# One transformer layer on one core: latent tokens first in the opening stage, adaLN rows and Strassen sums arranged otherwise, projection pieces dealt out otherwise

## The chip, the cores and the metric

One core of a Trainium2 chip runs the whole layer in one program. The metric is the device time of one execution in microseconds (us). The kernel before takes 1133.83 us (median of 3 runs, 1131.55 to 1134.39). About 0.3% (3.4 us) is what a measurement of this kernel can tell from no change.

## The reference, cut to what matters

```python
mod = silu(c) @ w_ada + b_ada                       # 1024 -> 6*1024; mod_c the same with c_ctx
sh1, sc1, gt1, sh2, sc2, gt2 = split(mod, 6)
hc = modulate(rmsnorm(ctx, g_pre_mix), csh1, csc1)  # 256 context tokens
hl = modulate(rmsnorm(x, g_pre_mix), sh1, sc1)      # 1024 latent tokens, width 1024
# hc, hl @ w_in -> z_q z_k z_v z_dec z_og z_f z_rx z_rg
#   states of the context: GLA (k, v, decay) and RG-LRU (conv of z_rx)
#   latents: bidirectional chunked GLA from those states | 2-D DFT of z_f | conv + RG-LRU of z_rx
x = x + gt1 * rmsnorm(yl @ w_out, g_post_mix)
hf = modulate(rmsnorm(x, g_pre_ffn), sh2, sc2)
x = x + gt2 * rmsnorm((silu(hf @ w_gate) * (hf @ w_up)) @ w_down, g_post_ffn)   # d_ff = 2816
```

All of it is float32. `modulate(h, sh, sc)` is `h * (1 + sc) + sh`.

## The kernel before, in words

Nearly all large products run as three float32r matmuls (`mm3`, lines 84 to 86): both operands are split into a rounded part (ScalarE cast) and a remainder (VectorE or GpSimd subtraction). The activations of the latents, normalised and modulated, stay in SBUF transposed, as `hl` (rounded and remainder, two halves of 512 tokens, 8 blocks of 128 features).

**Opening stage.** `ada_half` (L145) loads the shift and scale columns of `w_ada` in two halves of eight 512 KB loads each (pieces of 2 KB), multiplies them with the two conditioning vectors in four column groups of TensorE, and `columns` (L194) turns the result into per-feature columns. The context comes first: its k and v projections (`zkc`, `zvc`) and conv input (`zc`) run between the two halves. Then the first 512 latent tokens are modulated (`mod_half`), then the second 512, and the projections v, k, rx of the latents follow (`z_v0`, `z_k`, `z_rx`).

**Middle stage.** `gla_states(p)` makes the chunk states of a pair of heads; `gla_block(p, n)` is one of eight blocks of 128 tokens. `fill(n, mark)` (L752) issues n pieces of a queue of q and f projections behind a marked TensorE instruction; a piece is six matmuls of 512 columns, a whole projection of 512 tokens four pieces. `rg_gates` and `rg_scan` are the RG-LRU, `fourier` the DFT, `z_og` the output gate.

**Rows.** `ada_row` (L664) makes 1024 values of `mod` on VectorE: one step (`ada_step`) is a load of 512 KB and one multiply-add over 128x1024; after eight steps TensorE sums the partitions, into a row replicated on all partitions (`row_ps`), or, for the FFN shift, into a column.

**Border to the FFN.** `x_product` multiplies with `w_out`, normalises, and gives `xn`; `x_transposed` transposes it to `hx`. The FFN's gate and up products use seven Strassen products: `sums(n)` builds the five operands s1, s2, s4, s3, a22 of token block n, each split by `put` (L931; two casts and two subtractions of 256 columns). `first(f)` does the two products of feature block f that need no sums (24 matmuls of 512 columns); `rest(f)` the other five (60), on weights prepared by `t_split`. `EARLY` blocks have their `first` before `rest(0)`. Feature blocks are 22; then `down` runs.

**Order.** The tile framework orders each engine's instructions by its own planned timeline, starting from program order; `tc.issue_after` adds an edge behind a given instruction. SBUF is 43 pages of 4 KB a partition (`pg`) and 13 half pages (`hp`), given out in program order.

Of the kernel before, what the change touches and what calls it, by code (L numbers as in the profile page):

```python
# [16 lines left out]
P = 128  # L17
# [21 lines left out]
def tile_trunk(ctx: ExitStack, tc: tile.TileContext, A: dict):  # L39
# [101 lines left out]
    sp2, sm4 = sm("sp2", 4), sm("sm4", 4)
    V.tensor_scalar_mul(sp2, sp, 2.0)
    V.tensor_scalar_mul(sm4, sp, -4.0)

    def ada_half(h):  # L145

        ps = (aux if h else mm)("ada_ps")
        for k in range(KB):
            raw = pg((P, 2, 512), name="ada_raw")
            load(raw, A["w_ada"][k * P:(k + 1) * P, 0:2 * D].rearrange("p (i n) -> p i n", i=2)[:, :, h * 512:(h + 1) * 512])  # L150
            for i in range(2):
                for j in range(2):
# [41 lines left out]
    def columns(h, ps):  # L194

        sb = hp((P, 256), name="ada_sb")
        S.copy(sb, ps[:, 0:256])
        pc = (aux if h else mm)("ada_pc")[:, 0:16].rearrange("p (m q) -> p m q", q=8)
        for m in range(2):
            PE.matmul(pc[:, m], sb[:, m * P:(m + 1) * P], sel, start=True, stop=True)  # L200
        pcv = pc.rearrange("p m (i j w) -> p i j m w", i=2, j=2)

        def col4(c0):
            return sml[:, c0 + 4 * h:c0 + 4 * h + 4].rearrange("p (j m) -> p j m", j=2).unsqueeze(3).to_broadcast([P, 2, 2, 2])

        Av, Bv = (t[:, 4 * h:4 * h + 4, :].rearrange("p (j m) w -> p j m w", j=2) for t in (Acol, Bcol))
        V.tensor_add(Av, pcv[:, 1], col4(S_BSC))
        V.scalar_tensor_tensor(Av, Av, 1.0, col4(S_GPM), op0=ALU.add, op1=ALU.mult)
        V.tensor_add(Bv, pcv[:, 0], col4(S_BSH))

    load(cm, A["cmat"])
    cb = [row_block(A["ctx"], i * P) for i in range(2)]
    ada_ps = ada_half(0)
    for xb in cb:
        norm(xb)
    cT = list(transposed(cb))
# [74 lines left out]

    raws = w_N_load([(C_V, 256), (C_DEC, 32)])
    columns(0, ada_ps)
    hc = [[pg((P, 4, TC), F32R, f"hc{s}{i}") for i in range(2)] for s in range(2)]

    def mod_c(h):
        return modulate(cT[4 * h:4 * h + 4], 1, lambda kk: hc[0][kk // 4][:, kk % 4, :], lambda kk: hc[1][kk // 4][:, kk % 4, :])

    mod_c(0)
    w_v = [w_N_split(raws, G)]  # L300
    w_k_raw = [w_T_load(C_K)]
    zvc = [mm("zvc") for _ in range(2)]
    zkc = [mm("zkc") for _ in range(2)]

    def v_c(ks):
        for m in range(2):
            for k in ks:
                mm3(zvc[m][:, 0:288], *(hc[s][k // 4][:, k % 4, m * P:(m + 1) * P] for s in range(2)), *w_v[0][k], k == 0, k == KB - 1)

    v_c(range(4))  # L310
    ada_ps = ada_half(1)
    w_k_raw.append(w_T_load(C_K + P))
    w_k = [split(r, (P, KB, P), eng=G) for r in w_k_raw]
    xb0 = [row_block(A["x"], i * P) for i in range(2)]
    columns(1, ada_ps)
    started = mod_c(1)
    v_c(range(4, KB))
    for p in range(2):
        z_c(w_k[p], range(KB), zkc[p])
    w_rx_raw = w_T_load(C_RX)  # L320
    xb0 += [row_block(A["x"], i * P) for i in range(2, 4)]


    wdec_raw, wdec = hp(name="wdec_raw"), hp((P, 512), F32R, "wdec")
    load(wdec_raw, A["wdec"])
    with tc.issue_after(started.ins):
        S.copy(wdec, wdec_raw)
        V.tensor_sub(wdec[32:64, :], wdec_raw[32:64, :], wdec[32:64, :].bitcast(F32))
        w_rx = [split(w_rx_raw, (P, KB, P))]
        for xb in xb0:  # L330
            norm(xb)
# [33 lines left out]
    for m in range(2):  # L365
        v0_parts(zdt_c, m, vNc[0][:, m, :], zvc[m])
# [1117 lines left out]
```

## Time and profile before

| | |
|---|---|
| median of 3 runs | 1133.83 us |
| the profiled execution, its span | 1134.18 us, 1132.4 us |
| TensorE busy | 1078.5 us, 95% |
| VectorE, ScalarE, GpSimd busy | 72%, 43%, 7% |
| mean granted TensorE clock | 0.979 |
| chain of waits: TensorE's share | 83% |

A busy TensorE is not at its peak: the windows of the trace count a matmul that waits in the pipeline, or runs at half the clock, as busy. A window therefore has to be read with its granted clock beside it.

### The profile page before, as it was taken

What the parts mean: (1) busy time and instruction counts of PE and PEld (TensorE: products, weight loads), DVE (VectorE), ACT (ScalarE), POOL (GpSimd) and SP (SyncE); (2) the same over time, 40 slices, a digit from 0 to 9 for tenths busy, and PEclk for the clock granted to TensorE, in tenths of its full rate; (3) what the DMA queues carried; (4) which work ended last, traced back from release to release, by engine and by line L of the source; (5) the groups of instructions that cost most, each with busy time, mean ns of one, the idle gap of its engine ahead of it and who ended that gap; (6) DMA issues with size and microseconds to landing.
All of it is one profiled execution on the core that took longest, in us unless ns stands there. A gap on an engine that the chain in (4) does not pass through costs nothing.

```text
span 1132.4 us, 15040 instructions
## 1 busy us (share of the span) xinstructions
PE 1078.5 (95%) x5547; PEld 900.1 (79%) x5547; DVE 810.4 (72%) x1370; ACT 490.2 (43%) x931; POOL 83.6 (7%) x93
## 2 busy tenths in 40 slices
PE   4899998999899999959999999999999999999997
PEld 2799896776689888838878888888888888888886
DVE  3474698477588466797879777768777668967794
ACT  3452675466373355663314332333323247554251
POOL 2210000103100011370000000000000000000100
PEclk8899999999999999979999999999999999999999
DMA  9802312222427222361283242424232468767572
GB/s 328 306 20 67 120 38 56 48 56 71 167 75 243 75 93 94 112 167 57 93 276 106 78 136 84 121 75 139 85 114 81 157 218 315 267 216 231 181 283 75
DMA packets 119970, 156.42 MB, mean 138 GB/s; under 512 B 8276, under 2 KB 70996, under 8 KB 119896
## 3 DMA queue, kind: packets, MB, share of 16 engines
q1 hardware_dynamic: 106536, 128.72, 34.9%
q10 hardware_dynamic: 13360, 26.75, 7.0%
q8 instruction: 43, 0.70, 0.3%
q14 instruction: 31, 0.25, 0.1%
HBM read 124.50 MB, written 28.57 MB: 135 GB/s over the span
## 4 chain that ended last, share of the span: by engine, by line
PE 83%; DVE 6%; DMA 4%; ACT 3%; issue 2%; POOL 1%; SPq 0%; DVEq 0%; POOLq 0%; ACTq 0%
PE prod L84 11%; PE prod L85 11%; PE prod L86 11%; PE dn L85 6%; PE dn L84 6%; PE dn L86 6%; PE z L84 3%; PE z L85 3%; PE z L86 3%; PE o_ps L85 3%; PE o_ps L86 3%; PE o_ps L84 3%; PE zn L85 3%; PE zn L86 3%; PE zn L84 2%; DMA wraw<-in_w_in 2%
## 5 line engine op out<-in xcount | busy, mean ns | idle before, releaser
L85 PE MATMUL dn<-dr,dl 128*128 128x512 f32 (+1 forms) x319 | 121.8, 382 | 0.0
L86 PE MATMUL dn<-dr,dl 128*128 128x512 f32 (+1 forms) x319 | 121.8, 382 | 0.0
L84 PE MATMUL dn<-dr,dl 128*128 128x512 f32 (+1 forms) x319 | 118.7, 382 | 0.0
L85 PE MATMUL zn<-w_lo,hl 128*128 128x256 f32 (+1 forms) x256 | 74.1, 292 | 0.0
L84 PE MATMUL zn<-w_hi,hl 128*128 128x256 f32 (+1 forms) x256 | 73.2, 289 | 0.0
L86 PE MATMUL zn<-w_hi,hl 128*128 128x256 f32 (+1 forms) x256 | 72.9, 288 | 0.0
L84 PE MATMUL prod<-a,b_hi 128*128 128x512 f32 x176 | 69.5, 395 | 1.4 <-ACT b_hi L91 1.4
L84 PEld LDWEIGHTS dn<-dr,dl 128*128 128x128 f32 x319 | 60.0, 188 | 11.7
L85 PE MATMUL prod<-a,b_hi 128*128 128x512 f32 x176 | 69.3, 393 | 0.0
L86 PEld LDWEIGHTS dn<-dr,dl 128*128 128x128 f32 x319 | 60.0, 188 | 11.7
L85 PEld LDWEIGHTS dn<-dr,dl 128*128 128x128 f32 x319 | 60.0, 188 | 11.5
L84 PE MATMUL prod<-s,wb_hi 128*128 128x512 f32 x176 | 68.9, 391 | 0.0
L86 PE MATMUL prod<-s,wb_lo 128*128 128x512 f32 x176 | 68.5, 389 | 0.0
L85 PE MATMUL prod<-s,wb_hi 128*128 128x512 f32 x176 | 68.5, 389 | 0.0
L86 PE MATMUL prod<-a,b_lo 128*128 128x512 f32 x176 | 67.9, 390 | 0.0
L84 PE MATMUL z<-hl,w_hi 128*128 128x512 f32 x160 | 65.5, 409 | 1.0 <-ACT on L605 1.0
L85 PE MATMUL z<-hl,w_hi 128*128 128x512 f32 x160 | 64.0, 400 | 0.0
L86 PE MATMUL z<-hl,w_lo 128*128 128x512 f32 x160 | 63.8, 399 | 0.0
L1189 ACT CAST dl<-h 128x512 fp32r<-128x512 f32 x77 | 47.8, 620 | 35.7 <-issue 20.6
L1190 DVE TENSOR_TENSOR dl<-h,dl 128x512 fp32r<-128x512 f32 x77 | 53.3, 692 | 13.6 <-ACT dl L1189 13.6
L1122 ACT CAST b<-wf_raw 128x512 fp32r<-128x512 f32 x22 | 13.7, 622 | 113.6 <-PE prod L86 105.7
L85 PE MATMUL o_ps<-wo_lo,yh 128*128 128x512 f32 x128 | 49.9, 392 | 0.0
(368 smaller groups left out, 2800.8 us busy)
## 6 DMA issues: line engine op xcount, KB each, us to landing
ada_raw<-in_w_ada SPq DMA_DIRECT2D x48, 512.0 KB, 6.3
h<-hd SPq DMA_DIRECT2D x77, 256.0 KB, 5.0
wd_raw<-in_w_down SPq DMA_DIRECT2D x77, 256.0 KB, 4.8
hd<-c ACTq DMA_DIRECT2D x55, 256.0 KB, 2.0
wf_raw<-in_w_gate SPq DMA_DIRECT2D x25, 512.0 KB, 3.9
wf_raw<-in_w_up SPq DMA_DIRECT2D x22, 512.0 KB, 4.4
wraw<-in_w_in SPq DMA_DIRECT2D x16, 512.0 KB, 4.6
xb<-in_x SPq DMA_DIRECT2D x8, 512.0 KB, 8.1
```

The costliest lines, as they stand in the source:

```text
L84: PE.matmul(out, lh, rh, start=start, stop=False)
L85: PE.matmul(out, lh, rl, start=False, stop=False)
L86: return PE.matmul(out, ll, rh, start=False, stop=stop)
L1122: S.copy(hi, u[:, 4:8])
L1189: S.copy(t[:, 0, :], raw)
L1190: V.tensor_sub(t[:, 1, :], raw, t[:, 0, :].bitcast(F32))
```

## The change: what it does

- The four blocks of the first 512 latents are loaded first, on ScalarE's queue. `w_ada`'s shift and scale columns come in eight parts of 2 x 512 KB, by feature block (pieces of 512 bytes instead of 2 KB), with the k and rx weights between them. For each feature block: transposes, `ada_part`, `columns`, `modulate`, and one block of depth of the four k and rx products of the first half. The context comes after the latents' second half.
- Four pieces of q and f stand behind each pair's keys; between the blocks of pair 0 there are 2, 1, 2, 1 ... where there were two each; pair 1 keeps one each.
- The FFN scale becomes a column, applied with the shift on ScalarE in the transposition; `xn` is made on ScalarE. The steps of the rows are placed otherwise, and the last row (gt2) moves from block 3 to blocks 10 and 11 of the FFN.
- `sums` works in place, in two steps first and two later, all subtractions on VectorE; six `first` stand before `rest(0)` instead of three. `y_block` uses half pages.

```diff
+    xb0 = [pg(name="xb") for _ in range(4)]
+    for i, xb in enumerate(xb0):
+        nc.scalar.dma_start(xb, A["x"][i * P:(i + 1) * P, :])
...
+    def ada_load(b):
+        raws = []
+        for i in range(2):
+            raw = pg((P, KB, P), name="ada_raw")
+            c = i * D + b * P
+            load(raw, A["w_ada"][:, c:c + P].rearrange("(k p) n -> p k n", p=P))
+            raws.append(raw)
+        return raws
+
+    def ada_part(raws):
+        ps = aux("ada_ps")
         for k in range(KB):
...
             for i in range(2):
+                g = 32 * (2 * i + k % 2)
+                PE.matmul(ps[g:g + 32, 0:P], s32[:, k, :], raws[i][:, k, :], start=k < 2, stop=k >= KB - 2)
...
+    a_raw, w4_raw = {0: ada_load(0)}, {0: w4_load(0)}
+    for b in range(1, KB):
+        a_raw[b] = ada_load(b)
+        if b % 2 == 0:
+            w4_raw[b // 2] = w4_load(b // 2)
+    v_raws = w_N_load([(C_V, 256), (C_DEC, 32)])
...
+    def z_block(b):
+        for (hi, lo), ps in zip(w4, z4):
+            mm3(ps, hi[:, b, :], lo[:, b, :], hl[0][0][b // 2][:, b % 2, :], hl[1][0][b // 2][:, b % 2, :], b == 0, b == KB - 1)
...
+    for b in range(KB):
+        kps = [next(x0_T)]
+        columns(b, ada_part(a_raw.pop(b)))
+        modulate(kps, 0, lambda kk: hl[0][0][kk // 2][:, kk % 2, :], lambda kk: hl[1][0][kk // 2][:, kk % 2, :])
+        if b:
+            z_block(b - 1)
+        if b % 2:
+            w4_split()
+    softplus()
+    w_v = [w_N_split(v_raws)]
+    z_block(KB - 1)
...
+    def scale_column(ps):
+        g8 = hp((P, P), name="g8")
+        load(g8[0:KB, :], A["g_pre_ffn"].rearrange("(k p) -> k p", p=P))
+        PE.transpose(ps[:, 16:16 + KB], g8[0:KB, :], ident[0:KB, 0:KB])
+        V.tensor_copy(sc2, ps[:, 16:16 + KB])
+        V.scalar_tensor_tensor(sc2, ps[:, 0:KB], 1.0, sc2, op0=ALU.add, op1=ALU.mult)
...
-        yield from ada_row(4 * D, times_row("g_pre_ffn", 1.0))
-        yield from ada_row(3 * D, None)
+        yield from ada_row(4 * D, scale_column, False)
+        yield from ada_row(3 * D, shift_column, False)
...
     with tc.issue_after(mid.ins):
         z_q(0, 1)
+    fill(4, mid)
     rg_ctx()
...
     for n in range(4):
-        fill(2, gla_block(0, n))
+        fill(2 - n % 2, gla_block(0, n))
...
-    fill(3, mid)
+    fill(4, mid)
...
     z_rg(1)
-    ada_step(9)
+    ada_step(8)
...
     fourier(zf[0], 0)
-    ada_step(0)
+    ada_step(1)
...
-            V.scalar_tensor_tensor(xn[:, hs], xr[:, hs], r2, sc2[:, hs], op0=ALU.mult, op1=ALU.mult)
+            S.mul(xn[:, hs], xr[:, hs], r2)
...
-                S.activation(x[:, kk, :], ps[:, k * P:(k + 1) * P], AF.Identity, bias=sh2[:, kk:kk + 1])
+                S.activation(x[:, kk, :], ps[:, k * P:(k + 1) * P], AF.Identity, bias=sh2[:, kk:kk + 1], scale=sc2[:, kk:kk + 1])
...
+        put("a22", n, a22)
+        V.tensor_add(a22, a21, a22)
+        put("s1", n, a22)
         yield
+        V.tensor_sub(a21, a11, a21)
+        V.tensor_sub(a11, a22, a11)
+        put("s2", n, a11)
         yield
-        G.tensor_sub(s4, a12, s2)
-        put("s4", n, s4)
-        yield
-        G.tensor_sub(s3, a11, a21)
-        put("s3", n, s3, G)
-        yield
-        put("a22", n, a22, G)
...
+        V.tensor_sub(a12, a12, a11)
+        put("s4", n, a12)
+        put("s3", n, a21)
...
-    EARLY = 3
-    all_of(sums(1))
+    EARLY = 6
+    for _ in range(2):
+        next(s01[1])
     first(0)
...
-        if f == 3:
-            for _ in ada_row(5 * D, times_row("g_post_ffn", 0.0)):
-                pass
-            gt2 = rows[2]
+        if f == 10:
+            last_row = ada_row(5 * D, times_row("g_post_ffn", 0.0))
+            for _ in range(KB):
+                next(last_row)
+        if f == 11:
+            all_of(last_row)
+            gt2 = rows[1]
```

## Rows read from the trace of the kernel before

**Rows 1.** Windows: busy us (instructions) of PE, PEld, DVE, ACT, POOL; clock, DMA, GB/s.

```profile
0.00:20.00 20.00, 8.02 (x82) 4.51 (x83) 6.05 (x34) 5.67 (x9) 1.95 (x8) 1.00 0.93 324
20.00:40.00 20.00, 13.29 (x110) 9.86 (x109) 3.21 (x14) 6.83 (x11) 8.18 (x5) 0.74 1.09 359
40.00:60.00 20.00, 17.92 (x130) 17.72 (x129) 14.91 (x31) 12.51 (x24) 4.77 (x5) 0.83 0.65 216
...
260.00:280.00 20.00, 18.00 (x99) 12.67 (x98) 12.23 (x31) 15.62 (x38) 6.26 (x6) 1.00 0.23 70
...
300.00:320.00 20.00, 15.38 (x59) 9.03 (x57) 10.52 (x10) 10.67 (x13) 0.00 (x0) 0.91 0.29 96
...
480.00:500.00 20.00, 14.62 (x56) 10.96 (x54) 19.82 (x24) 14.56 (x43) 18.14 (x16) 0.83 0.62 178
500.00:520.00 20.00, 11.44 (x44) 9.32 (x45) 18.36 (x26) 8.23 (x14) 6.23 (x4) 0.74 0.24 58
...
580.00:600.00 20.00, 19.25 (x80) 14.58 (x80) 18.45 (x23) 5.84 (x8) 0.00 (x0) 1.00 0.80 262
...
sum 1133.00, PE 1078.45 PEld 900.14 DVE 810.40 ACT 490.16 POOL 83.63; mean PE 18.92 PEld 15.79 DVE 14.22 ACT 8.60 POOL 1.47
```

**Rows 2.** Windows cut to single stages, columns as in Rows 1.

```profile
4.00:14.00 10.00, 3.93 (x23) 2.79 (x24) 5.48 (x30) 3.79 (x7) 1.11 (x2) 1.00 1.03 379
...
498.00:504.00 6.00, 0.82 (x4) 0.36 (x2) 5.96 (x11) 2.57 (x6) 1.83 (x3) 0.80 1.19 294
...
186.00:198.00 12.00, 8.48 (x45) 6.56 (x44) 10.74 (x27) 10.85 (x20) 0.00 (x0) 0.85 0.25 66
...
690.00:730.00 40.00, 40.00 (x178) 33.13 (x177) 30.07 (x41) 12.79 (x17) 0.00 (x0) 1.00 0.37 111
```

**Rows 3.** TensorE's groups in 0:60; count, busy us and mean ns, idle before.

```profile
L181 PE MATMUL xT_ps<-cm,xb 128*128 128x128 f32 x39 | 6.8, 313 | 10.1 <-DVE xb L171 10.1
L84 PE MATMUL zvc<-w_hi,hc 128*128 128x288 f32 x16 | 6.6, 427 | 5.3 <-ACT w_hi L91 3.2 <-DVE hc L190 2.1
...
L84 PE MATMUL zkc<-hc,w_hi 128*128 128x256 f32 x16 | 5.4, 337 | 1.1 <-ACT w_hi L91 1.1
...
L84 PE MATMUL zc<-hc,w_hi 128*128 128x256 f32 x15 | 4.4, 293 | 0.0
```

**Rows 4.** Timeline of TensorE in the opening stage; start, us, idle before.

```profile
14.23 2.37 PE L154 MATMUL ada_ps<-ada_raw,s 128*32 128x256 f32 x40
...
38.00 0.61 PE L200 MATMUL ada_pc<-cm,ada_sb 128*128 128x8 f32 x4 [0.49 <-ACT ada_sb L197]
...
42.28 0.61 PE L84 MATMUL zvc<-w_hi,hc 128*128 128x288 f32 x1 [2.08 <-DVE hc L190]
```

**Rows 5.** The chain that ended last: transposes of latents.

```profile
74.53 0.87 PE xT_ps L181 x8
```

**Rows 6.** Timelines of all engines, 186:198, 300:311 and 472:512.

```profile
195.98 0.77 PE L595 MATMUL o<-St,qT 128*128 128x128 f32 x2 [1.61 <-DVE St L519]
...
302.93 3.92 DVE L671 SCALAR_TENSOR_TENSOR ada_acc<-ada_raw,s,ada_acc 128x1024 f32<-128x1024 f32 x3
306.90 3.68 PE L682 MATMUL row_ps<-ada_acc,cm 128*128 128x512 f32 x4 [4.62 <-DVE ada_acc L671]
...
310.38 3.63 PE L613 MATMUL gate_ps<-uT,gates 128*128 128x512 f32 x8
...
473.32 0.40 PE L84 MATMUL prod<-a,b_hi 128*128 128x512 f32 x1
...
508.56 0.79 PE L84 MATMUL prod<-s,wa_hi 128*128 128x512 f32 x1 [9.74 <-ACT wa_hi L91]
```

**Rows 7.** VectorE's groups over the whole span.

```profile
L92 DVE TENSOR_TENSOR b_lo<-wf_raw,b_hi 128x1024 fp32r<-128x1024 f32 x22 | 26.9, 1222 | 0.6
...
L937 DVE TENSOR_TENSOR s<-s,s 128x256 fp32r<-128x256 f32 x24 | 17.3, 759 | 0.0
...
L937 DVE TENSOR_TENSOR a<-hx,a 128x256 fp32r<-128x256 f32 x16 | 6.2, 422 | 4.8 <-ACT a L936 4.8
```

More of the change, by code (lines that the diff above doesn't have):

```diff
@@ L101, in tile_trunk @@
     cm = pool.tile([P, 6, P], F32, name="cm")
+    for i in (0, 5):
+        load(cm[:, i, :], A["cmat"][:, i, :])
     ident, wmask, Cd, Sd, ones = (cm[:, i, :] for i in range(5))
@@ L192, in modulate, with columns @@
         return i
[L194 to L216, printed above, removed]
+    def columns(b, ps):
+        sb = hp((P, P), name="ada_sb")
+        S.copy(sb, ps[:, 0:P])
+        pc = aux("ada_pc")[:, 0:4]
+        PE.matmul(pc, sb, sel2.rearrange("p i w -> p (i w)"), start=True, stop=True)
+        bias = sml[:, S_BSH:S_BSH + 16].rearrange("p (i k) -> p i k", i=2)[:, :, b:b + 1].to_broadcast([P, 2, 2])
+        V.tensor_add(shsc[:, b], pc.rearrange("p (i w) -> p i w", i=2), bias)
+        V.tensor_scalar(Acol[:, b, :], shsc[:, b, 1, :], 1.0, sml[:, S_GPM + b:S_GPM + b + 1], op0=ALU.add, op1=ALU.mult)
     def w_T_load(c0):
@@ L289, in z_N @@
                 i = 0
[L292 to L331, printed above, removed]
     hl = [[[pg((P, 2, 512), F32R, name=f"hl{s}{h}") for _ in range(4)] for h in range(2)] for s in range(2)]
@@ new lines, in tile_trunk @@
+    kTc, uTc = cx[:, 0:2, :], cx[:, 2:4, :]
+    for p in range(2):
+        ps = mm("zkc")
+        z_c(w_k[p], range(KB), ps)
+        S.copy(kTc[:, p, :], ps[:, 0:TC])
+    kTcs = hp((P, 2, TC), name="kTcs")
+    exchange(kTcs, kTc)
+    zdt_c = hp((P, 4, 96), name="zdt")
+    for m in range(2):
+        ps = mm("zvc")
+        for k in range(KB):
+            mm3(ps[:, 0:288], *(hc[s][k // 4][:, k % 4, m * P:(m + 1) * P] for s in range(2)), *w_v[0][k], k == 0, k == KB - 1)
+        v0_parts(zdt_c, m, vNc[0][:, m, :], ps)
@@ L407, in tile_trunk @@
+    dec_T(zdt_c, 2, zdec_c[0:96, :])
+    for blk in range(2):
+        ps = mm("zc")
+        z_c(w_rx[blk], range(KB), ps)
+        conv(ps[:, 0:TC], uTc[:, blk, :], blk, TC, TC)
     la_c = pg((P, 2, 2, TC), name="la_c")
@@ L775, in tile_trunk @@
     load(gates, A["gates"])
-    with tc.issue_after(mid.ins):
-        z_q(0, 1)
-    rg_ctx()
-    w_f = [w_T(C_F)]
     qT.append(pg(name="qT"))
@@ L806, in tile_trunk @@
     for n in range(6, 8):
-        fill(9, gla_block(1, n))
+        fill(1, gla_block(1, n))
+    fill(99, mid)
     w_rg.append(w_T(C_RG + P))
@@ L1109, in first @@
     def first(f):
-        p1, c11 = hp(name="p1"), hp(name="c11")
+        if f in (4, 5):
+            pair = pg((P, 2, 512), name="p1")
+            p1, c11 = pair[:, 0, :], pair[:, 1, :]
+        else:
+            p1, c11 = hp(name="p1"), hp(name="c11")
         S.copy(p1, prod(b1s[f], 0, "a11", mm))
@@ L1377, in tile_trunk @@
     for f in range(NFF):
-        new = begun < NFF and begun - f <= (EARLY if f < 2 else EARLY - 1)
-        if new:
-            ff_gate(begun)
-            ff_up(begun)
+        if f + 2 < NFF:
+            ff_gate(f + 2)
+            ff_up(f + 2)
         wn = t_split(f + 1) if f + 1 < NFF else None
@@ L1386, in tile_trunk @@
         rest(f, w)
-        if new:
+        if begun == f + 2 < NFF:
             ff_b1(begun)
```

203 lines of the change are left out of this document (114 added, 89 removed).

## The prediction

> **What bounds the kernel now.** I read the windows of 20 us first. TensorE is busy 1078.45 of 1132.4 us, so 54 us are idle, and they lie in a few places [rows 1]: 20.8 us in 0:60, 2.0 in 260:280, 4.6 in 300:320, 13.9 in 480:520, 0.75 in 580:600. The reader is to see the clock beside them: 0.74 and 0.83 in 20:60, 0.83 and 0.74 in 480:520. That is the lower level, 1.2 GHz, for part of the window; each time it came after TensorE had waited, and it doubles what a matmul takes. Everywhere else TensorE is full at 2.4 GHz: in 690:730, in the FFN, 178 matmuls of 512 columns take 40 us, 0.225 us each [rows 2], and since some records can be missing I use 0.222. So the kernel is bound by TensorE, its amount of work hardly changes here, and the change is worth what it takes out of these places.
>
> **Opening stage.** Matmuls of 256 columns are taken at half of 0.222 (0.111 us), of 288 at 0.125, a transposition at 0.87 / 8 = 0.11 [rows 5]. By 60 us the kernel before has done three times 16 `zvc`, three times 16 `zkc`, three times 15 `zc` and 39 transposes [rows 3]: 6.0 + 5.3 + 5.0 + 4.3 = 20.6 us of lasting work, beside w_ada's products. After the change the first half of the latents is done when all eight parts of w_ada are: 32 transposes and 96 matmuls of 512 columns, 3.5 + 21.3 = 24.8 us of lasting work. When is that?
> By DMA: the pieces of 512 bytes move slower. In 498:504, where weights come in such pieces and the engines are saturated, 294 GB/s flow; in 4:14, with w_ada in pieces of 2 KB, 379 [rows 2]. So 8.4 MB of w_ada take 28.5 us instead of 22. The latents' 2.1 MB take 5.7 at 370, the 2.1 MB of k and rx weights (1 KB pieces, between the two rates) 6.4. With 2 us ahead the last part lands at 43. Behind it stand the part's product, its column, the modulation and the last block of depth. In the kernel before it took 4.3 us from a column's matmul to the first matmul on its modulated tokens [rows 4]; with 1.9 for the 32 products (40 instructions took 2.37 [rows 4]) and 2.7 for 12 matmuls, the end is at 52.
> By TensorE: w_ada's products are now 256 instructions of 128 columns. At the price of the old ones of 256 columns (0.059 us) that is 15 us, halved with the columns 7.6; both ends are open. With 24.8 and about 2 for the columns, 34 to 42 us. The latents share the DMA with the first parts, so their transposes start near 17 us, with some 6 us of w_ada's products done by then: end at 45 to 53, and 3 us later for a slow start of the clock. I take 54 for both together, then 3 us for two new waits: all four banks change hands, and the second half of the latents (2.1 MB behind w_ada and the v weights, 4 + 6 us) is modulated only just before TensorE wants it. So 57 us at 24.8 us of work; the kernel before gets there at 60 + 4.2 = 64. The gain would be 7; I take 6, because VectorE now also does splits that GpSimd did (8 us in 20:40 [rows 1]). Bounds: -11 and +2. The context's work only moves.
> The DMA rate has a rule. The Trainium skill, "DMA: Bandwidth & Descriptors" (Why small descriptors are slow), gives each packet a fixed overhead of about 3 cycles; for 512 bytes that would be 19 cycles for 16, for 2 KB 67 for 64, an estimate of 13% more time. The two windows make it 29%. By the page w_ada would take 25 us instead of 28.5, the end would come 2 to 3 us earlier, and the total would be about 1106.
>
> **Middle stage.** In 186:198 TensorE is busy 8.48 of 12 us at a clock of 0.85 [rows 2]: it waits for the q halves that travel through a DMA and for states (until 195.98 [rows 6]). `fill(4, mid)` puts 4 pieces, 24 matmuls, 5.3 us of work, just there. It covers the 3.5 us idle, and with them perhaps the slow clock that follows; gain 3.5, bounds 0 and 6. These pieces are missing between the blocks: of 16 there, 10 are left (4 + 6), and block 3 of pair 0 has none. What blocks without pieces cost is seen at 260:280, the end of pair 1: 2.0 us idle in 20 [rows 1]. I take 1 lost in pair 0 (0 to 3) and 0.5 won in pair 1, which has two more pieces behind block 4. In all -3, bounds -6 and +3.
>
> **Rows.** At 302.3 TensorE waits 4.62 us for the multiply-adds of the FFN scale's row; the row's matmuls at 306.9 then run in a window with clock 0.91 [rows 1, 6]. The eight steps stay where they are, but the finishing matmuls come a whole DFT later, so the gate matmuls (3.4 us, at 310.38 [rows 6]) come forward. Next late is the split of the output gate's weights, behind the multiply-adds on VectorE: 306.9 + 1.2 [rows 6, 7] = 308.1, against gates done at 305.7: 2.4 us idle. Of 4.6 + about 1.5 for the clock, 3.5 are won; bounds 0 and 6, since a late load of `g8` would stop TensorE. The row gt2 does the same eight multiply-adds in blocks 10 and 11, where VectorE has as little room: -0.5 of the 0.75 idle in 580:600, bounds -1 and +1.
>
> **Border.** The first `first` starts at 473.3, and `rest(0)` begins at 508.6 after a wait of 9.74 us for a split weight [rows 6]. In between TensorE has three `first` and 8 transposes, 72 x 0.222 + 0.9 = 16.9 us, so 18.4 us are lost. VectorE is full, 19.82 and 18.36 of 20 us [rows 1], and does not run freely: a subtraction of 256 columns takes 0.759 us on the sums, with GpSimd busy 18.14 of 20, and 0.422 on a11 and a12, earlier, with GpSimd mostly idle [rows 1, 7].
> After the change VectorE has, behind 473: the last row block 2.9; sums, 13 additions at 0.69 (512 columns, between 0.422 for 256 and 1.222 for 1024 [rows 7]) and 28 to 34 subtractions at 0.422, 20.8 to 23.3; three weight splits at 1.222, 3.7; six additions of `first`, 4.1; `t_split(0)`, five at 0.69 and two splits, 5.9: 37.4 to 39.9 us. TensorE has six `first`, 32 + 0.9 us. So `rest(0)` begins near 473 + 38.5, and 5.6 us are lost instead of 18.4. In blocks 0 to 3 no `first` follows, TensorE needs 60 x 0.222 = 13.3 us a block, and VectorE (30.07 of 40 us at 18.7 a block, less 1.9 for what is missing) 12.1: tight, about 1 us lost. Gain 12. Bounds: -17 if the overlap of VectorE's instructions makes them cheaper than their means, -4 if pages are late (43 are just enough for seven operands, 28 pages, with six blocks begun). `xn` and the scale move from VectorE to ScalarE, which has room; `y_block` on half pages is cost at nothing: one product of 10.7 us covers it, and without that cover each of eight row blocks would wait for four transposes and a subtraction, 0.44 + 0.69 us.
>
> **Sum.** -6 - 3 - 3.5 - 0.5 - 12 = -25, on the profiled execution's 1134.18 us (1132.4 of span, 1.8 around it): 1109 us. It stands 0.35 above the median, which changes nothing.
>
> **Rivals.**
> 1. *The border stays bound*, by pages or VectorE: -4 instead of -12, 1117 us. For it: 37 to 40 us of VectorE against 33. Against: 0.422 is measured alone. Chance 0.2.
> 2. *The moved waits come back*: the planner puts the pieces elsewhere, or the split and `g8` take the row's place. The change then does not do there what it says: 1115.5. Chance 0.14.
> 3. *Nothing is late next*: the better bounds in opening and border, -11 and -17, 1099. Chance 0.08.
> 4. *Slower: the opening runs at 1.2 GHz.* w_ada now comes in eight portions about 5 us apart, and TensorE works in bursts between them. In 20:60 the clock fell after such waits to 0.74 and 0.83 [rows 1]. If it stays low, 34 to 42 us of work take 68 to 84, from about 12 us on; the first half ends at 80 to 95 instead of 54, and with 26 to 41 more the total is 1135 to 1150, say 1142. It decides from an end at about 79 on. Against it: at the low clock TensorE has 8 to 10 us of work for each portion of 5 us and does not wait any more. The Trainium skill's "TensorE: Matmul & The Clock Gate" (HAM oscillation) describes this case, short bursts between DMA waits that stay at the lower clock; this trace agrees only in that the clock fell after waits. Chance 0.06.
>
> **How the numbers follow.** The forecast has 0.52. Its own range, adding the bounds of the parts in part, is 1098 to 1124. The range to 1095 and 1128 takes in rivals 1 to 3 and leaves out rival 4 and ends where several bounds meet. Faster by over 0.3% (below 1130.4): all but rival 4 and a few cases in which opening and border both fail, 0.90; within 0.3%: 0.04; slower: 0.06.
>
> **What would show it.** Right: windows 0:60 with less than 15 us idle and a clock above 0.9 after 30 us; the span's windows around the first pair's blocks full; no wait of TensorE for `ada_acc`; less than 7 us between the end of the last `first` and the first product on s1, with the sums' subtraction near 0.42 us and GpSimd at rest. Wrong: the first half's k and rx products ending after 60 us, a wait for weight loads at the border, or new idle time between blocks of the middle stage over 5 us.

## The result, and the profile after

The changed kernel takes 1123.58 us (median of 4 runs, 1122.12 to 1125.55) against 1133.32 for the kernel before on the same chip: ratio 0.9917, 95% interval 0.9894 to 0.994. It is faster, by 10 us instead of the 25 forecast. The profiled execution took 1122.12 us (span 1120.3), the fastest of the four; that is 12.1 us less than the profiled one of before, and the parts below add up to that.

Windows of the changed kernel, columns as in [rows 1], each to be held against the same window there:

```profile
0.00:20.00 20.00, 6.42 (x54) 4.02 (x58) 7.99 (x41) 8.76 (x15) 3.04 (x10) 1.00 1.00 293
20.00:40.00 20.00, 19.33 (x183) 14.45 (x174) 8.88 (x17) 5.99 (x10) 0.00 (x0) 1.00 1.17 302
40.00:60.00 20.00, 18.16 (x168) 13.93 (x167) 9.95 (x22) 8.10 (x13) 0.55 (x1) 1.00 0.89 285
260.00:280.00 20.00, 18.05 (x104) 13.37 (x103) 12.02 (x29) 14.29 (x39) 6.96 (x6) 1.00 0.29 86
300.00:320.00 20.00, 18.09 (x107) 14.04 (x106) 13.04 (x17) 19.39 (x22) 1.09 (x3) 0.99 0.24 78
480.00:500.00 20.00, 13.97 (x53) 10.28 (x52) 17.48 (x40) 18.17 (x50) 0.00 (x0) 0.84 0.38 105
500.00:520.00 20.00, 18.57 (x81) 15.02 (x81) 16.52 (x28) 10.84 (x22) 0.00 (x0) 0.99 0.41 106
580.00:600.00 20.00, 20.00 (x90) 16.58 (x89) 13.77 (x20) 6.02 (x8) 0.00 (x0) 1.00 0.26 80
```

The reader sees the opening full from 20 us on, the row's wait in 300:320 cut by 2.7 us, block 3's gap in 580:600 gone, and the border (480:520) still with 7.5 us idle and a clock of 0.84. The windows do not show what a stage gained, since TensorE does other work in the same window. For that I take the starts of products that both kernels have. All times in us from the start of the span; "border" is rest(0)'s first product less the FFN's first product; the last column is the median of the kernel's runs (of e6, e7, e15 and e16 the one run). Kernels e1 to e16 are the experiments below. Every time but the last column comes from the one profiled execution of its kernel. In e1, e2, e5, e7 and e9 eight transpositions stand ahead of the FFN's first product that stand behind it in the others, so their border is to be read 0.8 to 0.9 us longer.

| | first v product of latents | first z_rg | first w_out product | FFN's first product | rest(0) | border | first down product | us |
|---|---|---|---|---|---|---|---|---|
| before | - | 278.4 | 378.0 | 473.3 | 508.6 | 35.2 | 915.9 | 1133.3 |
| changed | 61.3 | 276.4 | 372.8 | 470.2 | 515.7 | 45.5 | 903.8 | 1123.6 |
| e1 pieces as before | 60.8 | 276.4 | 372.3 | 470.5 | 513.7 | 43.2 | 901.7 | 1118.2 |
| e2 exchange early | 60.9 | 276.4 | 372.2 | 470.5 | 513.6 | 43.2 | 901.7 | 1120.2 |
| e3 y on pages | 61.1 | 276.5 | 372.9 | 468.1 | 513.1 | 45.0 | 901.3 | 1118.9 |
| e4 weights early | 61.1 | 277.0 | 373.4 | 470.8 | 514.1 | 43.3 | 902.2 | 1120.2 |
| e5 exponentials early | 61.4 | 281.7 | 377.5 | 475.8 | 520.1 | 44.3 | 908.3 | 1123.5 |
| e6 w_ada in 4 KB | 61.1 | 279.3 | 375.6 | 473.0 | 521.3 | 48.3 | 909.4 | 1127.7 |
| e7 few w_ada products | 55.4 | 272.3 | 366.6 | 464.9 | 507.8 | 42.9 | 895.9 | 1114.2 |
| e8 less on ScalarE | 59.9 | 275.3 | 371.6 | 469.0 | 512.8 | 43.7 | 902.5 | 1120.9 |
| e9 scans in halves | 61.8 | 273.3 | 365.9 | 464.1 | 507.9 | 43.8 | 895.9 | 1113.8 |
| e10 t_split first | 61.2 | 279.5 | 375.8 | 473.2 | 520.8 | 47.6 | 908.9 | 1124.4 |
| e11 = e1 + e3 | 60.7 | 276.2 | 372.1 | 469.7 | 514.5 | 44.9 | 902.7 | 1119.1 |
| e12 pieces before keys | 59.7 | 270.5 | 367.9 | 465.3 | 512.1 | 46.8 | 900.3 | 1119.9 |
| e13 = e3 + e9 + e12 | 60.8 | 266.7 | 363.4 | 458.6 | 506.9 | 48.2 | 895.0 | 1112.8 |
| e14 = e13 + e4 | 61.1 | 267.8 | 364.4 | 459.6 | 503.5 | 43.9 | 891.6 | 1109.9 |
| e15 no sums | 59.8 | 275.3 | 370.1 | 467.4 | 510.1 | 42.6 | 898.1 | 1116.4 |
| e16 short hx | 61.1 | 276.4 | 372.8 | 470.2 | 513.8 | 43.6 | 901.8 | 1120.2 |

Line by line between before and changed, with the forecast in brackets: the second half's k and rx products, before which both kernels have done the same work in another order, come 1.4 us earlier (6); the stage from there to z_rg gains 0.6 (3); from z_rg to the w_out product 3.1 (3.5); the w_out product loses 2.0 (0); from the FFN's first product to the first down product 9.0 are won (12.5). The sum is -12.1.

### The profile page after: what moved, and what is told of

Its sections match the earlier page's. It is cut to its first block, busy times and chain, and to the rows that moved or that the text cites. A ratio compares the mean times of both kernels' runs of the same rounds, so it can differ in the third digit from the quotient of the medians.

```text
span 1120.3 us, 15350 instructions
## 1 busy us (share of the span) xinstructions
PE 1078.3 (96%) x5696; PEld 903.5 (81%) x5696; DVE 796.2 (71%) x1394; ACT 505.2 (45%) x953; POOL 43.2 (4%) x64
## 4 chain that ended last, share of the span: by engine, by line
PE 85%; DVE 5%; SPq 3%; ACT 3%; DMA 2%; issue 2%; POOL 1%; DVEq 0%; POOLq 0%; ACTq 0%
PE prod L86 12%; PE prod L84 12%; PE prod L85 12%; PE dn L85 6%; PE dn L86 6%; PE dn L84 6%; SPq L70 3%; PE zn L86 3%; PE zn L84 3%; PE zn L85 3%; PE o_ps L84 3%; PE o_ps L86 3%; PE o_ps L85 3%; PE z L84 2%; PE z L85 2%; PE z L86 2%
## 5 line engine op out<-in xcount | busy, mean ns | idle before, releaser
L85 PEld LDWEIGHTS dn<-dr,dl 128*128 128x128 f32 x319 | 60.0, 188 | 11.7
L84 PEld LDWEIGHTS dn<-dr,dl 128*128 128x128 f32 x319 | 60.0, 188 | 11.7
L84 PE MATMUL z<-hl,w_hi 128*128 128x512 f32 x160 | 62.5, 415 | 7.0 <-ACT on L645 4.9
L85 PE MATMUL z<-hl,w_hi 128*128 128x512 f32 x160 | 63.8, 399 | 0.0
L1192 ACT ACTIVATE c<-c 128x512 f32<-128x512 f32 x22 | 13.9, 634 | 88.5 <-DVE c L1191 85.3
```

The lines of the kernel that those rows point to most:

```text
L84: PE.matmul(out, lh, rh, start=start, stop=False)
L85: PE.matmul(out, lh, rl, start=False, stop=False)
L1192: S.activation(c21, c21, AF.Silu)
```

## The experiments

### Opening: transfers or TensorE's order

TensorE in the changed kernel's opening (timeline: start, duration, idle before):

```profile
13.85 0.64 PE L168 MATMUL ada_ps<-ada_raw,s 128*32 128x128 f32 x2
15.20 0.47 PE L196 MATMUL xT_ps<-cm,xb 128*128 128x128 f32 x1 [0.71 <-DVE xb L186]
15.60 1.93 PE L168 MATMUL ada_ps<-ada_raw,s 128*32 128x128 f32 x30
...
19.38 1.94 PE L168 MATMUL ada_ps<-ada_raw,s 128*32 128x128 f32 x32
...
23.17 1.92 PE L168 MATMUL ada_ps<-ada_raw,s 128*32 128x128 f32 x28
25.03 1.33 PE L84 MATMUL z<-hl,w_hi 128*128 128x512 f32 x3
```

The first part of w_ada has begun to be used at 13.85, but the fourth transpose, and what stands behind it, waits for the norms of the latents until 15.2. Three parts are multiplied at half clock (1.93 us for 30; full clock is granted from 25.9), and the first k product comes at 25.0. From there to 61.3 TensorE is nearly full at 2.4 GHz. So either the transfers or this order could set the end.

e6 reads w_ada's columns in large pieces, e7 leaves out most of its products:

```diff
 e6
-            load(raw, A["w_ada"][:, c:c + P].rearrange("(k p) n -> p k n", p=P))
+            load(raw, A["w_ada"][b * P:(b + 1) * P, i * D:(i + 1) * D].rearrange("p (k n) -> p k n", k=KB))
 e7
-        for k in range(KB):
+        for k in range(KB - 2, KB):
```

> The changed kernel with the eight parts of w_ada's shift and scale columns read in pieces of 4 KB instead of 512 bytes: the same bytes, but other rows of the matrix, so the values are not the layer's. It takes away the slow small pieces alone. Forecast's step (the end of the first half is set by the DMA rate and a tail of 9 us): the transfers shrink by about 6 us, the first v product, which stands right behind the first half, comes at 54 to 56 us instead of 61.3. Theory: TensorE has 36 us of work in order from its first k product at 25.0 on, and before that the chain of latents, norms, column and split sets the start; then the first k product comes at 22 to 25 and the first v product at 58 to 61.

> The changed kernel with a quarter of w_ada's products in the opening (4 instructions of 128 columns for each part instead of 32); the shift and scale are then wrong. Transfers, latents and the k and rx products are as in the changed kernel. Theory (TensorE's own order and work set the end of the first half): 3/4 of 256 instructions go, about 120 at 0.034 us behind the first k product and 72 at 0.064 (half clock) before it; the first v product comes at 53 to 57 us instead of 61.3. Rival (the DMA sets it): the last part lands near 44 to 45 as before and the end stays at 59 to 61.

The same window of the changed kernel and then of e6 (last columns: clock, DMA share, GB/s):

```profile
20.00:30.00 10.00, 9.62 (x84) 7.01 (x75) 4.72 (x8) 2.96 (x5) 0.00 (x0) 1.00 1.18 301
```

```profile
20.00:30.00 10.00, 9.62 (x76) 7.01 (x69) 4.62 (x8) 2.70 (x5) 0.00 (x0) 1.00 1.03 400
```

The reader is to see 400 instead of 301 GB/s beside the same 9.62 us of TensorE. The opening's transfers end 8 us earlier in e6 (a load of w_ada's last part lands at 36.2 instead of 44.1), and the first v product comes at 61.1 instead of 61.3: the small pieces cost nothing. With fewer products (e7) it comes at 55.4, 5.9 us earlier, at unchanged transfers (43.4 for the same load), although full clock is granted only from 29.6 there. TensorE's own order sets the opening. Small pieces are slow all the same: 33% more time for a byte in this window, in which some weights come in pieces of 1 KB in both kernels. The Trainium skill, "DMA: Bandwidth & Descriptors" (Why small descriptors are slow), gives about 3 cycles for a packet, from which 19/16 against 131/128, an estimate of 16%, would follow for 512 bytes against 4 KB; the windows make it twice that.

### Middle: where the pieces are short

In the changed kernel pair 0's keys are covered: pair 1's key transposes begin at 222.3 instead of 234.1, with two pieces (2.7 us) fewer done. But then TensorE waits. Its timeline, first of the kernel before, where those transposes follow without a wait, then of the changed kernel:

```profile
234.10 1.03 PE L509 MATMUL k_tr<-cm,Kt 128*128 128x128 f32 x8
```

```profile
222.30 0.66 PE L549 MATMUL k_tr<-cm,Kt 128*128 128x128 f32 x4 [0.17 <-DVE Kt L537]
226.97 1.31 PE L549 MATMUL k_tr<-cm,Kt 128*128 128x128 f32 x6 [4.02 <-DVE Kt L534]
...
254.34 0.63 PE L84 MATMUL z<-hl,w_hi 128*128 128x512 f32 x1 [2.94 <-ACT on L645]
```

Both waits are followed by 3.4 us at half clock (from 227.3 and 254.6). The kernel before and e1 have neither of them. e1 deals the pieces out as before, e2 begins the key exchange before the last four blocks of pair 0, e5 also the exponentials, e12 puts four pieces ahead of the key transposes:

```diff
 e1
-    fill(4, mid)                      # behind pair 0's keys: gone
-        fill(2 - n % 2, gla_block(0, n))
+        fill(2, gla_block(0, n))
-    fill(4, mid)                      # behind pair 1's keys
+    fill(3, mid)
 e2, e5 (ahead of blocks 4 to 7)
+    kt_begin(1)
+    gs1 = [gla_exp(1, d) for d in range(2)]    # e5 alone
...
 e12
+    queue += [f_steps(blk, h) for blk in range(2) for h in range(2)]
...
+        fill((2, 1, 2, 4)[n - 4], gla_block(0, n))
-    fill(4, mid)
+    fill(1, mid)
```

> The changed kernel with the pieces of q and f dealt out as before (none behind pair 0's keys, two between all its blocks, three behind pair 1's keys). Theory: the four pieces behind pair 0's keys won about 7 us there (its stage ends at 222 instead of 234 us, with 2.7 us less of pieces done), and pair 1 gave about 7 us back, since its key exchange has no pieces left to lie behind. Then this kernel loses and wins the same: pair 1's key transposes start near 233, z_rg near 277 (changed kernel 276.4), the time is 1122 to 1124. Rival: the dealing out is worth the 3 us forecast: z_rg near 279.5, 1125 to 1127.

e1's z_rg is at 276.4 as in the changed kernel: the dealing out gained nothing in the stage, as the theory has it. Its time is lower than either theory gave, in part by a cause elsewhere: with the eight transpositions reckoned in, its border is 1.4 us shorter, because the planner wrote another order there, and e2 has the same order and the same border. The profiled executions of e1 and of the changed kernel differ by 2.1 us, the medians by 5.4; the rest lies in executions without a profile (two of e1's four had a mean granted clock of 0.994, its profiled one 0.991), and its cause is open.

> The changed kernel with pair 1's key exchange begun four blocks earlier. Theory: TensorE's waits of 4.0 us before pair 1's key transposes and 2.9 us later come from the exchange's transfer (9 to 10 us from its issue to the transposes) and from nothing else; they go, z_rg starts near 272 instead of 276.4, and the time is 1116 to 1119. Rival: the keys' exponential and product on ScalarE and VectorE (VectorE is busy 18.1 of 20 us in 220:240) set the time, not the exchange: the transposes wait as before, z_rg at 275.5 to 276.5, 1121 to 1123.

The theory fell: z_rg at 276.4. TensorE waited for VectorE's `am` (1.79 us) and then for the keys' product (2.56 us).

> The changed kernel with pair 1's key exchange, exponentials and products of keys (gla_exp) issued ahead of the last four blocks of pair 0, instead of behind them. The exchange alone did nothing: TensorE still waited for VectorE (busy 9.5 of 10 us in 220:230 and 2.7 of 10 in 210:220). Theory: the exponentials stand behind block 7 in the order of ScalarE and VectorE, and this order is the wait; with them in the idle stretch before, the waits of 4.2 us at pair 1's key transposes go, z_rg starts near 271 to 273 instead of 276.4, the time is 1116 to 1119. Rival: pair 1's end is set elsewhere (TensorE's waits at 251 and 273 for a bank that GpSimd's power behind a scan frees); then what is won here is lost there, z_rg at 275.5 to 276.5, the time 1120 to 1123.

That fell too, and lost 5 us: pair 0's blocks now wait behind the exponentials, and 218.4 to 232.1 runs at half clock.

> The changed kernel with four pieces of f ahead of pair 1's key transposes (behind block 7 of pair 0) and one behind them, instead of one and four. Neither an earlier exchange nor earlier exponentials took the wait of 4.2 us at those transposes away; the products of keys on VectorE end near 225.6 us whatever stands before. Theory: TensorE is short of work there and only there, so pieces put ahead of the transposes cover the wait and the half clock behind it: 3 to 6 us, z_rg at 270.5 to 273.5 instead of 276.4, the time 1117 to 1120. Rival (a wait for states or banks takes its place, as at pair 0's blocks in the kernel before): the chunk states come behind the pieces, blocks 0 to 2 of pair 1 wait for them, z_rg at 275.5 to 277.

This holds. TensorE in e12:

```profile
224.65 0.60 PE L549 MATMUL k_tr<-cm,Kt 128*128 128x128 f32 x4
225.53 1.31 PE L549 MATMUL k_tr<-cm,Kt 128*128 128x128 f32 x10 [0.28 <-DVE Kt L534]
```

The wait is 0.28 instead of 4.02 us, without the half clock. z_rg comes at 270.5, 6.0 us earlier; 1.6 of that were already there in the opening, so 4.4 belong to the stage. The keys are hardly earlier: TensorE has other work until they come. A landmark has its own spread, though: the code up to z_rg but for the opening is the same in the changed kernel, e3, e4, e6, e8, e10, e15 and e16, and z_rg comes between 275.3 and 279.5 there, late where half clock also fell at 200 (e6, e10).

The second wait, at 254.34, is for a bank. On VectorE, GpSimd and TensorE in the changed kernel:

```profile
250.80 2.34 DVE L697 TENSOR_TENSOR_SCAN a<-a,h,ti 128x1024 f32<-128x1024 f32 x1
250.97 2.65 POOL L121 TENSOR_TENSOR ors<-orst,mhalf 128x2 f32<-128x2 f32 x1 [20.69 <-DVE orst L119]
...
253.88 0.69 POOL L121 TENSOR_TENSOR ors<-orst,mhalf 128x2 f32<-128x2 f32 x1 [0.25 <-DVE orst L119]
```

GpSimd's power of two columns takes 0.69 us, and 2.65 beside a scan of 2.34 us. Without it the attention block is not normalised, and its bank is not free for the next piece. (The expectation of e9 says that all kernels have this wait; the kernel before and e1 do not.) e9 halves the scans:

```diff
-        V.tensor_tensor_scan(fl(a, d), fl(a, d), fl(ti, d), h0[...], ...)
+        for i in range(2):
+            cs = slice(i * 512, (i + 1) * 512)
+            V.tensor_tensor_scan(fa[:, cs], fa[:, cs], ft[:, cs], fa[:, 511:512] if i else h0[...], ...)
```

> The changed kernel with each latent RG-LRU scan of 1024 columns done as two of 512. In all kernels so far TensorE waits 3.1 us at about 251 us and 2.1 us at about 274 for a bank that the normalisation of an attention block frees; GpSimd's power for it takes 2.65 us there, beside a scan of 2.34 us on VectorE, and 0.69 us otherwise. Theory: the power stands still while the scan runs, so with scans half as long it takes about 1.5 us; z_rg starts 1 to 2.5 us earlier, at 274 to 275.5 instead of 276.4, the time is 1120 to 1122 at the same border. Rival: the power or the multiplications before and behind wait for VectorE's whole work, not for one instruction: power 2.3 us or more, z_rg as before or later.

The same instructions in e9:

```profile
251.67 1.28 DVE L700 TENSOR_TENSOR_SCAN a<-a,h,ti 128x512 f32<-128x512 f32 x1
251.84 1.59 POOL L121 TENSOR_TENSOR ors<-orst,mhalf 128x2 f32<-128x2 f32 x1 [21.41 <-DVE orst L119]
...
253.51 1.28 DVE L700 TENSOR_TENSOR_SCAN a<-a,ti 128x512 f32<-128x512 f32 x1
```

The power takes 1.59 us, as long as the shorter scan plus 0.3: GpSimd stands still for one instruction of VectorE. TensorE's waits of 2.94 and 1.95 us shrink to 0.93 and 0.22; z_rg comes 3.2 us earlier. The w_out product comes 6.9 us earlier, and the other 3.7 are won at the DFT: in the changed kernel its fold on VectorE stands behind a scan and TensorE waits for it, with half clock from 319.4 to 322.8 behind the wait; in e9 VectorE does the fold between the half scans, and TensorE does not wait for it:

```profile
319.24 3.60 PE L890 MATMUL Z_ps<-cm,zfold 128*128 128x128 f32 x16 [1.91 <-DVE zfold L873]
```

```profile
314.11 1.95 PE L893 MATMUL Z_ps<-cm,zfold 128*128 128x128 f32 x16
```

This second gain is one of order, and e13, which has the half scans too, does not keep it. At 1113.8 us e9 is the best single edit, more than I gave it. The Trainium skill, "SBUF — State Buffer" (SBUF: two separate sides), has VectorE and GpSimd share one port pair under an exclusive lock for a whole instruction, where the VectorE instruction has two inputs in SBUF and the GpSimd one reads SBUF. 2.65 beside 2.34 and 1.59 beside 1.28 agree, and so does a power at 285.39 in the changed kernel that takes 0.69 us beside a VectorE instruction of 0.69 with one input in PSUM.

### The w_out product: half pages

Three consecutive matmuls of the changed kernel, and of e3, where `y_block` is back on whole pages:

```diff
-        yh, yl = ([hp((P, 4, P), F32R, nm) for _ in range(2)] for nm in ("yh", "yl"))
+        yh, yl = ([t[:, 0:4, :], t[:, 4:8, :]] for t in (pg((P, KB, P), F32R, "yh"), pg((P, KB, P), F32R, "yl")))
```

> The changed kernel with y_block on whole pages as before. In the changed kernel the matmuls of the w_out product start every 0.233 us, in the kernel before every 0.228, with no wait longer than 0.1 us in either; 384 of them make the 2.0 us lost there. Theory: it comes with the place of y on half pages. Then the interval is 0.228 here, the stage from the first w_out product to the first gate product 95.4 instead of 97.4 us, the time 1119 to 1121. Rival 1: it comes with ScalarE's new work (xn and the scale): 0.233 and 97.4 as in the changed kernel, 1122. Rival 2: the interval differs from execution to execution: then other runs with half pages will show 0.228 too.

```profile
463.19 0.40 PE L84 MATMUL o_ps<-wo_hi,yh 128*128 128x512 f32 x1
463.42 0.40 PE L85 MATMUL o_ps<-wo_lo,yh 128*128 128x512 f32 x1
463.66 0.40 PE L86 MATMUL o_ps<-wo_hi,yl 128*128 128x512 f32 x1
```

```profile
463.14 0.39 PE L86 MATMUL o_ps<-wo_hi,yl 128*128 128x512 f32 x1
463.37 0.39 PE L84 MATMUL o_ps<-wo_hi,yh 128*128 128x512 f32 x1
463.59 0.39 PE L85 MATMUL o_ps<-wo_lo,yh 128*128 128x512 f32 x1
```

The step is 0.233 us against 0.227, the stage 97.4 against 95.2. The mean interval is 227.2 to 227.8 ns in the five kernels with whole pages (before, e3, e11, e13, e14) and 233.1 to 233.3 in the thirteen others. 384 matmuls times 5.5 ns are the 2.1 us. No wait and no clock shows it. Whether the address of the half page or its neighbours make it is open.

e11 undoes this and the pieces together:

> The changed kernel with two parts undone together: the dealing out of the pieces and y_block on half pages. Singly they gave 1118.2 (of which the stage itself 0, and 2.3 at the border, where the planner wrote another order) and 1118.9 us (2.1 in the w_out product). Theory: the two add up where they act: matmul interval 0.2275 in the w_out product, z_rg at 276.4, rest(0) 43 us behind the first product of the FFN, 1115.5 to 1117.5. Rival: the gain of the first was an accident of the border's order: 1118 to 1121.

The interval and z_rg came as expected, but not the time: a wait of 2.0 us for `yh` at 408.7 ate the gain of the pages, and the border took 44.9 us, not 43.

### Border: VectorE or ScalarE

TensorE's waits at the border in the changed kernel, and ScalarE's work ahead of the second (the load of these weights was issued at 476.76 and such a load takes about 4 us):

```profile
486.81 1.27 PE L1083 MATMUL x_tr<-cm,xn 128*128 128x128 f32 x8 [1.92 <-ACT xn L1075]
...
494.16 0.79 PE L84 MATMUL prod<-a,b_hi 128*128 128x512 f32 x1 [3.31 <-ACT b_hi L91]
...
497.02 0.80 PE L86 MATMUL prod<-a,b_lo 128*128 128x512 f32 x1 [0.79 <-DVE b_lo L92]
...
515.68 0.50 PE L84 MATMUL prod<-s,wa_hi 128*128 128x512 f32 x1 [1.43 <-ACT wa_hi L91]
```

```profile
490.06 1.97 ACT L977 CAST s<-hx 128x256 fp32r<-128x256 f32 x6
491.90 0.66 ACT L1160 ACTIVATE c<-c 128x512 f32<-128x512 f32 x1
492.43 0.73 ACT L977 CAST s<-hx 128x256 fp32r<-128x256 f32 x2
493.03 1.07 ACT L91 CAST b_hi<-wf_raw 128x1024 fp32r<-128x1024 f32 x1
```

ScalarE has no idle time from 482.6 until b_hi: it is casting the sums. The clock is at half from 493.5 to 500.3, and TensorE is busy for 5.4 us of that, so it costs another 2.7 us. The last wait, for wa_hi, is VectorE's: ScalarE is idle ahead of that cast, until `t_split` has formed its input:

```profile
514.58 1.04 ACT L91 CAST wa_hi<-wf_raw 128x1024 fp32r<-128x1024 f32 x1 [3.34 <-DVE wf_raw L1173]
```

Of the 7.5 us of waits ScalarE has 5.2 (xn, b_hi) and VectorE 2.2 (b_lo, wa_hi).

```diff
 e4   (and in e14)
     first(0)
+    ff_gate(3)
+    ff_b1(3)
     for s in s01:
         all_of(s)
 e8   (last block's xn, half of hx of the last two blocks)
+                V.tensor_scalar_mul(xn[:, hs], xr[:, hs], r2)
+                    V.tensor_scalar(x[:, kk, :], ps[...], sc2[...], sh2[...], op0=ALU.mult, op1=ALU.add)
 e10
+    w = t_split(0)
     all_of(s_last)
     first(4)
-    w = t_split(0)
 e15
-        V.tensor_add(a22, a21, a22)    # and the other three of sums
 e16
+                S.copy(x[:, 4 * g:4 * g + 4, :], ps.rearrange("p (k t) -> p k t", k=4))
```

> The changed kernel with the load and the split of the fourth gate weights put ahead of the second parts of the sums. Its cast waits at 493.0 us behind ScalarE's casts of the sums although its data have been there since about 481, TensorE waits 3.3 us for it and runs at half clock for the next 7 us. Theory (the order of ScalarE's work is the bound): this wait and the half clock go, the last of the five s1 products' start comes forward, rest(0) at 510 to 512 instead of 515.7, the time 1117 to 1119. Rival 1 (pages): the sums' operands wait for pages instead, no gain, 1121 to 1123. Rival 2 (VectorE's total): the wait moves to the split behind the sums, rest(0) not before 514, 1120.5 to 1122.

The wait moved on to the next weights (2.79 us at 500.19), the half clock was halved, border 43.3: the second rival's place, a gain of 2.2 us, against 1.4 in e1 and e2, where only the order differs.

> The changed kernel with less of ScalarE's work at the border: xn of the last row block, and scale and shift of half of hx of the last two blocks, on VectorE. ScalarE is busy 18.2 of 20 us in 480:500, and TensorE waits there for its xn and its b_hi; VectorE is busy 17.5 there and 9.7 of 10 in 490:500. Theory (ScalarE's new work, xn and the casts in a queue, is what is late next at the border): rest(0) begins 2 to 4 us earlier, 41 to 43 us behind the first product of the FFN instead of 43.2 to 45.5, the time is 1117 to 1120. Rival (VectorE's total is the bound): its work grows by 3 us, rest(0) begins 46 us or more behind, the time 1122 to 1125.

Neither: 43.7. The waits are longer, 8.6 us in sum, and VectorE's (2.60 for `xn`, 2.61 for `b_lo`, 3.38 for `wa_hi`); what makes the border shorter is that no half clock falls in it.

> The changed kernel with t_split(0) ahead of the last parts of the last sums, so that the first product on s1 needs less of VectorE's work before it. Theory (at the border VectorE and ScalarE together are full, and what stands last in their order sets rest(0)): the waits of 1.2 to 3.5 us for wa_hi go, rest(0) begins 1 to 4 us earlier, 41 to 44 us behind the FFN's first product instead of 45.5, and the time is 1118 to 1121. Rival: VectorE's total decides; the wait turns up behind rest(0)'s first product or at a split of b1, rest(0) not earlier in the sum, the time within 1 us of the changed kernel's 1122 to 1125.

The wait for wa_hi shrank from 1.43 us to 0.78. The border of 47.6 is not the edit's: two stretches ran at half clock, and in e6, where the border's code is untouched, the clock fell at the same two places, with the same waits for `xn`, `b_hi` and `b_lo` (1.93, 3.07, 1.80 us), and the border took 48.3. Against that the edit won 0.7 us. The rival is nearer.

> The changed kernel without the 16 additions and subtractions that form the operands of the sums (the puts stay, so the five products run on other values than the layer's): about 10 us less on VectorE between 470 and 515, nothing else changed. Theory of the forecast (VectorE's 37 to 40 us of work set rest(0)): rest(0) comes 35 to 38 us behind the FFN's first product instead of 45.5, the border's loss falls to 1 to 4 us. Theory from the trace (ScalarE's casts, hx and xn in one queue are late before VectorE is): rest(0) still 41 to 44 us behind, with the waits for xn and b_hi as before.

> The changed kernel with hx of the last two row blocks copied in two instructions of 512 columns instead of eight activations of 128 (scale and shift are left out there): about 3.4 us less on ScalarE at the border. Theory (ScalarE's queue is the bound): the waits for xn and b_hi of 2.1 and 3.5 us shrink by 2 to 4 us together, with them the half clock, rest(0) 40 to 43 us behind the FFN's first product instead of 45.5. Theory of the forecast (VectorE sets it): the waits move to b_lo and wa_hi, rest(0) 43.5 us or more behind.

TensorE's waits in e15, where VectorE has 10 us less to do, and in e16:

```profile
483.41 1.27 PE L1083 MATMUL x_tr<-cm,xn 128*128 128x128 f32 x8 [1.27 <-ACT xn L1075]
492.00 0.74 PE L84 MATMUL prod<-a,b_hi 128*128 128x512 f32 x1 [4.57 <-ACT b_hi L91]
```

```profile
493.16 0.50 PE L84 MATMUL prod<-a,b_hi 128*128 128x512 f32 x1 [4.12 <-ACT b_hi L91]
496.50 0.80 PE L86 MATMUL prod<-a,b_lo 128*128 128x512 f32 x1 [1.58 <-DVE b_lo L92]
```

e15 decides against the forecast: with VectorE relieved the border is still 42.6 us, VectorE's two waits are gone, and TensorE waits for ScalarE alone, 5.8 us. e16 takes the wait for `xn` away, not the one for `b_hi`, which stands behind casts in ScalarE's order, and then VectorE is late as well. So ScalarE's queue of casts is late first, and VectorE's work comes close behind it. What a relief is worth is not shown: the border's code is the same in the changed kernel, e6, e7 and e12, and its border took 43.8 (e7, with the eight transpositions) to 48.3 us (e6), by the planner's order and by where half clock fell. The 43.3 to 43.7 of e4, e8 and e16 lie hardly below that; only e15's 42.6 is a little clearer.

### The causes taken away together

> The changed kernel with three causes taken away together: scans in halves, four pieces of f ahead of pair 1's keys, y_block on whole pages. Theory: they act in different stretches and add up: z_rg at 267 to 269 us (singly 273.3 and 270.5 against 276.4), matmul interval 0.2275 in the w_out product, 2.1 us less there, and about 3.5 between z_rg and the w_out product; the time is 1106 to 1111. Rival: pieces and scans cover the same waits of pair 1; then z_rg stays at 269.5 to 271 and the time is 1110 to 1114.

The landmarks came as the theory has them (z_rg 266.7, interval 0.2275, the w_out stage 95.3), the time did not: from z_rg to the w_out product it took 96.6 us instead of e9's 92.7, with a wait of 3.2 for the DFT's fold on VectorE, and the border took 48.2 with 10.2 us at half clock, as in e6.

> As the run with three edits, and the fourth gate weights' load and split ahead of the second parts of the sums. Singly that moved TensorE's wait from the fourth to the fifth weights and halved the stretch at half clock (3.4 instead of 6.8 us), rest(0) 43.3 us behind the FFN's first product. Theory (the two engines are full, only the place of the wait changes): within 2 us of the run with three edits, better by 0 to 2 where the clock holds. Rival: it frees the border: 3 us or more better.

2.9 us better, between what the two gave. Part of it is the clock: 6.8 us at half clock at the border instead of 10.2. TensorE's waits at e14's border:

```profile
476.21 1.73 PE L1085 MATMUL x_tr<-cm,xn 128*128 128x128 f32 x8 [1.93 <-ACT xn L1077]
489.31 0.50 PE L84 MATMUL prod<-a,b_hi 128*128 128x512 f32 x1 [2.05 <-ACT b_hi L91]
490.85 0.80 PE L86 MATMUL prod<-a,b_lo 128*128 128x512 f32 x1 [0.33 <-DVE b_lo L92]
503.47 0.50 PE L84 MATMUL prod<-s,wa_hi 128*128 128x512 f32 x1 [0.93 <-ACT wa_hi L91]
```

e14 beats both kernels: 1109.93 us (1109.53 to 1111.1, 5 runs), ratio to the kernel before 0.9796 (0.9782 to 0.9809).

## Why the prediction was wrong, step by step

The direction was right and the size was not: 12.9 us of the forecast are missing on the profiled executions, 4.6 in the opening, 2.4 in the middle, 0.4 in the rows, 2.0 in the w_out product, 3.5 at the border. No single step makes the miss; the largest parts are the start of the opening and ScalarE at the border. Two of the forecast's own signs of being wrong came: the first half's k and rx products ended at 61.3, after 60, and new waits of 7.0 us lie between the middle's blocks. The third did not: the border's waits are for casts of weights, not for their loads.

- **Opening: the mis-sized term.** The end of the first half, 52 by DMA, 45 to 53 by TensorE and 54 for both together, became 61. The DMA was forecast well (300 GB/s; w_ada's last part landed just after 44.1, forecast 43), but it does not count (e6). TensorE's amount of work came out at the upper end of the forecast's 34 to 42 us: 36 us from 25.0 to 61, and 11 busy before that, most of it at half clock. Wrong was its start: I let it begin near 17 with 6 us of w_ada's products done; at 17.5 one part of eight was done and at 25 three, at half clock and behind norms, column, modulation and split. Rival 4 was at work there, until 25.9 and not after: then the granted clock stayed at its upper level until 227.3.
- **Middle: the gain was there, and came back.** 3.5 us at pair 0's keys was too low, about 7 were won. But I priced the missing pieces by 260:280 [rows 1], an end without key transposes. What they had hidden was pair 1's keys (4.0 us, then half clock), and the pieces behind pair 1's keys stand on the wrong side of the wait (e12). A wait of 2.9 us for a bank, with half clock behind it, came at 254 as well; halving the scans takes it away (e9).
- **Rows: the size right, the place not.** 3.1 of 3.5, with the next wait 2 us long as forecast, but at the DFT's fold and not at the gate's weights: that the two are of one length is luck. gt2's move took block 3's idle time away.
- **w_out product: cost at nothing, cost 2.1.** I bounded `y_block` by waits that its cover hides. None came; every matmul became 2.4% longer.
- **Border: the step that failed.** VectorE's 37.4 to 39.9 us were to set rest(0), with 5.6 lost; 11.7 were lost (45.5 less 33.8 of work). VectorE's durations were right (0.42 for a subtraction, GpSimd at rest), and so was its sum: it was busy 38.0 us from 470 to 516. That `xn` and the scale move to ScalarE, "which has room", was not: I never summed ScalarE for the border. It was at 14.56 of 20 us in 480:500 [rows 1] and came to 18.17, in a fixed order with the weights' casts at its end. Its waits are 5.2 of the 11.7 us lost, VectorE's 2.2 and the half clock behind them about 2.7, which was not in the sum either. The sum also took 0.222 us for a matmul, where the lines show steps of 0.227, and eight transpositions in the border of before, where there are sixteen.

## What to carry to other kernels

Sum every engine over the stretch in which a change puts work, the one that takes over included, and in its order: a cast that is last in a full queue stops TensorE although its data lie there. Work that fills a wait is worth its place, not its amount: pieces behind the waiting instruction left the wait of 4.0 us as it was, three of them moved ahead of it won 4.4 us. And a moved buffer is not free because its waits are hidden: look at the interval between two matmuls as well.

## What was not expected of the hardware

- A small instruction on GpSimd beside a scan on VectorE lasts as long as that: 0.69 us alone, 1.59 beside a scan of 1.28, 2.65 beside one of 2.34. It held a bank of TensorE.
- With y on half pages the step of the w_out matmuls was 0.233 us, with y on whole pages 0.227, in all 18 profiled executions.
- Executions of the same code differ in where the clock falls, and their times with it: e10 took 1121.2, 1123.5, 1125.3 and 1127.5 us at mean granted clocks of 0.992, 0.989, 0.988 and 0.986. In the opening full clock was granted at 20.4 to 21.2 us in three profiled executions (e8, e12, e15: first v product at 59.7 to 59.9) and at 25.3 to 27.4 in the others that do the same work there (60.7 to 61.8).
- A small edit far upstream gave the planner another order at the border, worth 1.4 us (e1, e2). Differences of that size between two such kernels say nothing of the edit.
